# Spreading sample steps over two tiles with deeper buffer rings in a hybrid decoder layer on eight cores

The kernel runs on all 8 cores of one Trainium2 chip (two dies, cores 0 to 3 and 4 to 7); every core does its own share and no core talks to another. The metric is the device time of the slowest core, in microseconds (us). Executions come in two states: in the slow one a whole die has a lower granted TensorE clock (0.84 to 0.89 instead of 0.97 in the slow runs of the changed kernel) and the program takes 1580 to 1630 us instead of 1480.

## What is computed

One layer of a decoder, for a long prompt (one sequence of 2048 tokens for each core) and for a group of short samples (16 sequences of 4 tokens for each core), with the same weights:

```python
def decoder_layer(x, mk, mv, s0, buf, pos0, p):
    mix, s_new, buf_new = token_mix(rmsnorm(x, p['norm_mix_g']), s0, buf, pos0, p)   # gated linear attention + pooling
    h = x + mix
    h = h + cross_attn(rmsnorm(h, p['norm_x_g']), mk, mv, p['w_xq'], p['w_xo'])      # 256 memory tokens, 4 heads
    h = h + sq_relu_mlp(rmsnorm(h, p['norm_mlp_g']), p['w_up'], p['w_down'])         # 1024 -> 4096 -> 1024
    return h, s_new, buf_new
# reference(...): once for the prompt (fresh state, K/V computed from mem_prompt),
# once for the samples (state_gla, state_pool, cache_mem_k, cache_mem_v are inputs)
```

For each sample a core has to load and update one recurrent state (0.5 MiB in f32, stored back), and to load one block of keys and one of values (1 MiB each in f32, 0.5 MiB once cast to bf16).

## The kernel before

The prompt goes through in four tiles of 512 tokens. Each tile has a first part (input projections, a chunk loop for the linear attention, pooling, branch gates, output projection), the attention over the memory, and the channel mixer (eight "up" and eight "dn" units). Weights are units of 1024 x 512. They pass through five slots, `wt0` to `wt4`; a unit that comes from the f32 input `wu` is cast by its load, which POOL issues; a unit that has once been stored in bf16 (`wscratch`) is loaded plain by SP:

```python
        if name in ONCE:
            cast, store = True, False
        elif times == 0 and name[:2] != "bp":              # first use of the unit
            cast, store = True, idx % 3 == 0
        elif times == 1 and idx % 3 != 0 and name[:2] != "bp":   # second use
            cast, store = True, True
        else:
            cast, store = False, False
        if cast:
            self.dma("pool", flat, src, nb=5.6)
        else:
            self.dma("sp", flat, self.scr[idx], nb=2.5, rtok=[("scr", idx)])
        if store:
            self.dma("sp", self.scr[idx], flat, nb=2.5, wtok=[("scr", idx)])
```

The work on the samples is three generators: G (states), K (keys), V (values). The prompt's code calls `self.step("G")` and so on at chosen places; each call emits one sample's work there. Before, they were called as follows, and each used a ring of two buffers:

```python
        # up(c): after each up unit            self.step("G"); self.step("K")
        # down(c): after each token block      self.step("G"); self.step("K")
        # end of the tile                      self.drain("G"); self.drain("K")
        # first part: after each v, k, q group  self.step("V")
    def states(self):
        ...
        for i in range(SB):
            sf = self.ring("s0f", self.s0f)              # two buffers
            sb_ = self.ring("s0b", self.s0b)
            ...
            self.dma("sp", sf[...], I["sgla"][i], nb=1.4)
            self.dma("pool", sb_[...], I["sgla"][i], nb=1.4)   # the same state again, cast
            ...                                          # matmuls; sf = sf * decay + k^T v on DVE
            self.dma("sp", O["sgs"][i], sf[...], nb=1.4)
            yield
    def keys(self):                                      # values(): the same with "cv"
        for i in range(SB):
            kv = self.ring("kv", self.kv)                # two buffers
            self.dma("pool", kv[:, :], I["ckT"][i], nb=3.0)
            ...
            yield
```

The instruction streams are not written in program order. A list scheduler in the kernel simulates the five engines with the given costs and puts each engine's instructions in the order in which they start there; on the chip every engine then takes its list in that order.

Of the kernel before, what the change touches and what calls it, by code (L numbers as in the profile page):

```python
# [37 lines left out]
class Graph:  # L38

    def __init__(self, nc, stack, dry):  # L40
        self.nc = nc
        self.stack = stack
        self.dry = dry
        self.ops = []
        self.n = 0
        self.base = {}
        self.byname = {}
        self.banks = {}
        self.blkcache = {}
        self.lastw = {}  # L50
        self.readers = {}
        self.tokw = {}
        self.tokr = {}
        self.pri_off = 0
        self.coarse = []

# [40 lines left out]
    def op(self, eng, fn, reads=(), writes=(), cost=0.1, dma=False, nb=0, rtok=(), wtok=(), tab=None):  # L97
        i = self.n
        self.n += 1
        if self.dry:  # L100
            return i
        deps = {}

        def add(j, kind):
            if j != i:
                o = deps.get(j)
                if o is None or kind < o:
                    deps[j] = kind
        rb = set()
        for ap in reads:  # L110
            rb.update(self.blocks(ap))
        wb = set()
        for ap in writes:
            wb.update(self.blocks(ap))
        for t in rtok:
            rb.add(("t", t))
        for t in wtok:
            wb.add(("t", t))
        lastw, readers = self.lastw, self.readers
        for b in rb:  # L120
            w = lastw.get(b)
            if w is not None:
                add(w, 0)
            if isinstance(b, tuple) and b[0] == "p":
                for r in readers.get(b, ()):
                    if self.ops[r].eng != eng:
                        add(r, 1)
        for b in wb:
            w = lastw.get(b)
            if w is not None:  # L130
                add(w, 1)
            for r in readers.get(b, ()):
                add(r, 1)
        for b in wb:
            lastw[b] = i
            readers[b] = []
        for b in rb:
            if b not in wb:
                readers.setdefault(b, []).append(i)
        o = Op()  # L140
        o.i, o.eng, o.fn, o.deps, o.cost, o.dma, o.nb, o.tab = i, eng, fn, deps, cost, dma, nb, tab
        o.pri = i + self.pri_off
        o.succ = []
        o.ev = None
        self.ops.append(o)
        return i

    def schedule(self, window=600):
# [23 lines left out]
        while left:  # L172
# [34 lines left out]
            if o.dma:  # L207
                s = max(t + c + 1.2, dma_free)
                dma_free = s + o.nb
                o.end = dma_free + 0.8  # L210
            else:
                o.end = t + c
# [258 lines left out]
class Prog:  # L471
# [50 lines left out]
    def alloc(self):  # L522
# [37 lines left out]
        self.s0f = [g.sb(f"s0f{i}", Q + 16384 + 4096 * i, [128, 4, 256], F32) for i in range(2)]  # L560
# [36 lines left out]
        self.kv = [g.sb(f"kv{i}", Y + 9216 + 4096 * i, [128, 2048], BF16) for i in range(2)]  # L597
# [69 lines left out]
    def W(self, name):  # L667
# [14 lines left out]
        if name in ONCE:  # L682
            cast, store = True, False
        elif times == 0 and name[:2] != "bp":
            cast, store = True, idx % 3 == 0
        elif times == 1 and idx % 3 != 0 and name[:2] != "bp":
            cast, store = True, True
        else:
            cast, store = False, False
        if cast:  # L690
            self.dma("pool", flat, src, nb=5.6)
        else:
            self.dma("sp", flat, self.scr[idx], nb=2.5, rtok=[("scr", idx)])
# [88 lines left out]
    def vcost(self, eng, out, ins, simple):  # L782
        n = self.nfree(out)
        if eng == "pool":
            return 0.2 + 0.00184 * n
        if simple and not any(self.is_ps(i) for i in ins):
            return 0.13 + 0.00063 * n
        return 0.13 + 0.00109 * n
# [38 lines left out]
    def dma(self, q, out, in_, nb=None, rtok=(), wtok=()):  # L827
        if nb is None:
# [3 lines left out]
                         cost=0.75 if q == "pool" else 0.07, dma=True, nb=nb, rtok=rtok, wtok=wtok)  # L832
# [9 lines left out]
    def consts(self):  # L842
        I = self.I
        d = self.dma
        for t, n in ((self.cols, "cols"),):
            d("sp", t[:], I[n][:, :])
        d("sp", self.bmk[:], I["c_bmk"][:, :])
# [24 lines left out]
    def consts4(self):  # L872
        I = self.I
        d = self.dma
        d("pool", self.smask[:], I["c_smask"][:, :])
# [5 lines left out]
    def program(self):  # L881
        I = self.I
        self.consts()
        self.gen = {}
        self.pend = None
        for s in range(4):
            self.dma("sp", self.land[s][:, :], I["xp"][s * 128:(s + 1) * 128, :])
        for s in range(4):
            self.norm_in(s)
# [12 lines left out]

    def norm_in(self, s):
        self.xnn = getattr(self, "xnn", {})
        self.xnn[s] = None
# [52 lines left out]
    def tile(self, ti):  # L958
# [4 lines left out]
        self.hooks = {}  # L963
        if ti >= 1:
            self.sample_hooks(ti)
        us = [(ti * 4 + s) % 5 for s in range(4)]
        b = self.bank()
        self.mm(self.pb[b][:16, :], [(self.wgz[:, kc, :], A[:, kc, :]) for kc in range(8)])
        self.cp("act", self.gzT[:, :], self.pb[b][:16, :])
        self.hook("gz")  # L970
        if first:
            self.consts2()
        u = self.W("v0")

        def vgroup(u, n, s):
# [3 lines left out]
            self.step("V")  # L979
        vgroup(u, 0, 0)  # L980
        for h in range(4):
# [10 lines left out]
        for s in range(1, 4):  # L992
            vgroup(u, 0, s)
        self.hook("v", 0, u)
        u = self.W("v1")
        for s in range(4):
            vgroup(u, 1, s)
        self.hook("v", 1, u)
        for nm, dst, E in (("k", self.kd, self.E1), ("q", self.qi, self.E2)):
            u = self.W(nm)  # L1000
            for h in range(4):
# [3 lines left out]
                self.step("V")  # L1005
            self.hook(nm, u)
        og = [self.W("og0"), self.W("og1")]
        u0 = self.W("u0")
        if first:
            self.consts3()  # L1010
            self.gen["pre"] = self.precompute()
# [17 lines left out]
        for c in range(4):  # L1029
# [47 lines left out]
            pend = (o2, c)  # L1077
            if first:
                self.step("pre", 2)
# [3 lines left out]
        for s in range(4):  # L1083
            uproj(u1, 1, s)
            if s == 1:
# [23 lines left out]
        if first:  # L1109
            self.consts4()  # L1110
        for n in range(2):
            ug = self.W(f"gb{n}")
            uw = self.W(f"bp{n}")
            for m in range(4):
# [6 lines left out]
                self.stt("dve", self.t1[:, m, :], t[:, :], 1.0, self.pb[b2][:, :], ALU.add, ALU.mult)  # L1121
            self.hook("b", n, ug, uw)
# [4 lines left out]
            for m in range(4):  # L1127
# [8 lines left out]
                self.tt("dve", self.mT[:, n * 4 + m, :], t2[:, :], self.t1[:, m, :], ALU.add)  # L1136
            self.hook("a", n, ug, uw)
            if first:
                self.step("pre", 4)
        if first:  # L1140
            self.drain("pre")
        for s in range(4):
# [18 lines left out]
        def C_(s):  # L1161
# [14 lines left out]
            for hp in range(2):  # L1176
                self.tt("pool", Pn[:, 2 * hp:2 * hp + 2, :], pf[hp][:, :].rearrange("p (h m) -> p h m", m=256),
# [23 lines left out]
        for f, s in ((O_, 0), (O_, 1), (O_, 2), (T_, 0), (O_, 3), (T_, 1), (C_, 0), (T_, 2), (C_, 1), (T_, 3), (C_, 2), (PT_, 0),  # L1201
                     (C_, 3), (X_, 0), (PT_, 1), (X_, 1), (PT_, 2), (M_, 0), (X_, 2), (PT_, 3), (M_, 1), (X_, 3), (M_, 2)):
            f(s)
            if f is O_ and s == 3:
                self.hook("o", uo)
        hs = {}
# [6 lines left out]
        def up(c):  # L1213
            h = hs[c] = self.ring("hid", self.hid)
            for j in range(2):
# [19 lines left out]
                self.step("G")  # L1235
                self.step("K")

        def down(c, each=None):
            h = hs[c]
            ud = [self.W(f"dn{c}_0"), self.W(f"dn{c}_1")]  # L1240
            for s in range(4):
# [7 lines left out]
                self.step("G")  # L1249
# [26 lines left out]
        if ti == 0:  # L1276
            self.drain("P")
        down(2, nxt)
        down(3, last)
        self.drain("G")  # L1280
# [201 lines left out]
    def states(self):  # L1482
# [22 lines left out]
        for i in range(SB):  # L1505
            sf = self.ring("s0f", self.s0f)
# [4 lines left out]
            self.dma("pool", sb_[:, :, :].rearrange("p h v -> p (h v)"), I["sgla"][i], nb=1.4)  # L1511
# [26 lines left out]
    def keys(self):  # L1538
# [14 lines left out]
        for i in range(SB):  # L1553
            kv = self.ring("kv", self.kv)
            kT = kv[:, :].rearrange("p (j m) -> p j m", m=256)
            self.dma("pool", kv[:, :], I["ckT"][i], nb=3.0)
# [28 lines left out]
    def values(self):  # L1585
        I = self.I
        bo = self.hold(1)[0]
        for i in range(SB):
            kv = self.ring("kv", self.kv)
            vv = kv[:, :].rearrange("p (a d) -> p a d", d=1024)  # L1590
            self.dma("pool", kv[:, :], I["cv"][i], nb=3.0)
# [93 lines left out]
```

## Time and profile before

| | before |
|---|---|
| median of all 20 runs (5 of them slow), us | 1594.3 |
| profiled fast run, spans of the cores | 1566.7 to 1607.8 |
| slowest core in it | core 6 |

The page of the profile gives busy times and the make-up of the chain of work that ended last.

```profile
PE 1360.1 (85%) x7848; PEld 664.3 (41%) x7848; DVE 642.1 (40%) x1105; ACT 462.6 (29%) x931; POOL 207.2 (13%) x284
...
PE 64%; DMA 25%; DVE 3%; issue 3%; ACT 2%; POOL 1%; SPq 1%; POOLq 0%; DVEq 0%; ACTq 0%
```

Read it so: TensorE (PE) is busy 85% of the span, and a quarter of the chain is transfers, which end the idle time of PE. Where that quarter lies is in the lines that the prediction shows.

For the comparison I cut each core's span at matmuls that every version has: the first matmul on the gate columns (`wgz`), the first matmul of each tile's attention (on `WqK`), and the first 384-column "up" matmul of each tile.

### The profile page before, as it was taken

The page shows a single profiled execution, that of the slowest core. Times are in us where ns is not written, and L with a number is a line of the kernel's source. Part 1 is how long each engine was busy: PE and PEld are TensorE (multiplying, and loading weights), DVE is VectorE, ACT ScalarE, POOL GpSimd, SP SyncE. Part 2 cuts the span into 40 slices and gives each one's busy share as a digit, 9 for nine tenths or more (in the row PEclk, how much of TensorE's full clock was granted, in tenths as well). Part 3 has the DMA queues.
Part 4 walks back from the last instruction along what each step waited for, and adds up shares of the span by engine and source line. Part 5 has one row for each costly group of instructions (what it writes and reads, how often), then busy time and mean ns, then how long its engine had stood idle before and what let it go on. Part 6 is the DMA issues. An engine that isn't in the chain of part 4 may idle for free.

```text
span 1607.8 us, 21667 instructions; the slowest of 8 cores (1566.7 to 1607.8 us)
## 1 busy us (share of the span) xinstructions
PE 1360.1 (85%) x7848; PEld 664.3 (41%) x7848; DVE 642.1 (40%) x1105; ACT 462.6 (29%) x931; POOL 207.2 (13%) x284
## 2 busy tenths in 40 slices
PE   0883988999999989973889999999977369999997
PEld 0341533444445435431334545444433235454443
DVE  1361233543545235532365523534415033354334
ACT  1251321522246216210115512521114033152111
POOL 3121010300102003100010200300111121020000
PEclk9997999999999999985889999999988679999887
DMA  9969799769894797889976314445879833411321
GB/s 210 171 130 192 152 217 183 184 131 174 219 225 143 195 203 237 192 211 247 225 247 216 129 53 137 126 137 191 190 131 255 146 104 145 158 53 70 114 105 60
DMA packets 49252, 265.59 MB, mean 165 GB/s; under 512 B 6294, under 2 KB 6750, under 8 KB 25452
## 3 DMA queue, kind: packets, MB, share of 16 engines
q0 software_dynamic: 18336, 93.77, 36.0%
q1 hardware_dynamic: 30812, 170.43, 29.9%
q8 instruction: 65, 1.06, 0.3%
q14 instruction: 39, 0.32, 0.1%
HBM read 302.31 MB, written 56.36 MB: 223 GB/s over the span
## 4 chain that ended last, share of the span: by engine, by line
PE 64%; DMA 25%; DVE 3%; issue 3%; ACT 2%; POOL 1%; SPq 1%; POOLq 0%; DVEq 0%; ACTq 0%
PE pb L725 58%; DMA wt_45<-wu 4%; PE pb L736 3%; DMA pmf<-wpmT 2%; DMA kv_131<-cv 2%; PE pb L755 2%; DMA kv_131<-ckT 2%; DMA sgs<-s0f_85 2%; DMA wt_46<-wu 2%; DMA wt_43<-wscratch 2%; DMA s0f_84<-sgla 2%; DMA wscratch<-wt_46 1%; DMA wt_43<-wu 1%; PE pb L746 1%; DMA s0b_116<-sgla 1%
## 5 line engine op out<-in xcount | busy, mean ns | idle before, releaser
L791 DVE TENSOR_TENSOR xh<-pb,xh 128x512 f32<-128x512 f32 x160 | 110.3, 690 | 140.1 <-PE pb L725 139.8
L791 POOL TENSOR_TENSOR stat<-stat,ncols 128x1 f32<-128x1 f32 (+2 forms) x87 | 59.2, 686 | 569.5 <-DVE stat L797 569.5
L779 ACT ACTIVATE tmp_86<-pb 128x512 f32<-128x512 f32 (+2 forms) x66 | 38.8, 588 | 249.1 <-PE pb L725 219.6
L725 PE MATMUL pb<-actT,wt_46 128*128 128x512 bf16 (+2 forms) x472 | 102.3, 372 | 3.2 <-DVE actT L791 2.2
L725 PE MATMUL pb<-actT,wt_45 128*128 128x512 bf16 (+2 forms) x408 | 89.1, 369 | 4.1 <-DVE actT L791 2.8
L725 PE MATMUL pb<-actT,wt_44 128*128 128x512 bf16 (+2 forms) x376 | 81.5, 369 | 8.3 <-DMA wt_44<-wu 4.5
L779 ACT ACTIVATE tmp_88<-pb 128x512 f32<-128x512 f32 (+2 forms) x67 | 39.4, 587 | 169.6 <-PE pb L725 126.2
L725 PE MATMUL pb<-actT,wt_43 128*128 128x512 bf16 x320 | 73.2, 385 | 0.0
L725 PEld LDWEIGHTS pb<-actT,wt_46 128*128 128x128 bf16 x472 | 45.0, 98 | 56.2 <-issue 10.2
L725 PE MATMUL pb<-actT,wt_47 128*128 128x512 bf16 (+2 forms) x312 | 65.5, 363 | 2.1 <-DVE actT L791 1.5
L725 PE MATMUL pb<-wt_43,actT 128*128 128x512 bf16 x224 | 56.2, 404 | 10.0 <-DMA wt_43<-wscratch 9.1
L779 ACT ACTIVATE tmp_89<-pb 128x512 f32<-128x512 f32 (+2 forms) x59 | 34.6, 586 | 97.6 <-PE pb L725 84.9
L779 ACT ACTIVATE tmp_87<-pb 128x512 f32<-128x512 f32 (+2 forms) x58 | 34.0, 586 | 94.9 <-PE pb L725 79.1
L725 PEld LDWEIGHTS pb<-actT,wt_45 128*128 128x128 bf16 x408 | 38.4, 98 | 48.1 <-issue 8.0
L725 PE MATMUL pb<-WqK,actT 128*128 128x512 bf16 x256 | 57.9, 379 | 0.0
L725 PEld LDWEIGHTS pb<-actT,wt_44 128*128 128x128 bf16 x376 | 35.4, 98 | 48.6 <-issue 10.4
L755 PE MATMUL pb<-ident,xn_90 128*128 128x128 bf16 x176 | 14.6, 231 | 48.2 <-DVE xn_90 L797 28.5
L725 PEld LDWEIGHTS pb<-actT,wt_43 128*128 128x128 bf16 x320 | 31.5, 99 | 38.4 <-issue 4.6
L725 PE MATMUL pb<-wt_47,hid_59 128*128 128x512 bf16 x192 | 46.7, 389 | 0.0
L725 PE MATMUL pb<-wt_44,actT 128*128 128x512 bf16 x192 | 44.2, 379 | 0.2 <-DVE ogs_93 L802 0.2
L725 PEld LDWEIGHTS pb<-actT,wt_47 128*128 128x128 bf16 x312 | 29.0, 98 | 34.0 <-issue 3.0
L791 DVE TENSOR_TENSOR actT<-pb,cols 128x1024 bf16<-128x1024 bf16 x32 | 38.9, 1218 | 9.3 <-PE pb L755 9.3
(466 smaller groups left out, 2350.6 us busy)
## 6 DMA issues: line engine op xcount, KB each, us to landing
wt_46<-wscratch SPq DMA_DIRECT2D x18, 1024.0 KB
wt_45<-wscratch SPq DMA_DIRECT2D x17, 1024.0 KB
wt_44<-wscratch SPq DMA_DIRECT2D x16, 1024.0 KB
wt_47<-wscratch SPq DMA_DIRECT2D x16, 1024.0 KB
wt_43<-wscratch SPq DMA_DIRECT2D x15, 1024.0 KB
wt_43<-wu POOLq DMA_DIRECT2D x14, 1024.0 KB, 16.5
wt_44<-wu POOLq DMA_DIRECT2D x14, 1024.0 KB, 15.9
wt_45<-wu POOLq DMA_DIRECT2D x14, 1024.0 KB, 15.1
```

What stands on the lines that cost most here:

```text
L725: ins = e.matmul(out, l, r, start=(start and i == 0), stop=(stop and i == m - 1))
L736: ins = e.matmul(out, l, r, start=(i == 0), stop=(i == m - 1))
L746: ins = e.matmul(out, l, r, start=False, stop=last and k == len(al) - 1)
L755: ins = e.transpose(o, i, d)
L779: return self.g.op("act", lambda e: e.activation(out=out, in_=in_, func=func, scale=scale, **kw), reads=rd, writes=wr, cost=c, tab=tab)
L791: return self.g.op(eng, lambda e: e.tensor_tensor(out=out, in0=in0, in1=in1, op=op), reads=[in0, in1], writes=[out], cost=self.vcost(eng, ...
```

## The change

The intent is to take the sample transfers off the path that sets the end: each ring gets four to six buffers in place of two, and their steps are spread, so that a transfer has the time of several steps. Its core, shortened:

```diff
-        self.s0f = [... 2 buffers]
+        self.s0m = [... 4 buffers]          # in the mixer of tile 1
+        self.s0a = [... 4 buffers]          # in the first part of tile 2
-        self.kv = [... 2 buffers]
+        self.kvm = kv + [3 more]            # keys
+        self.kva = kv + [4 more]            # values
...
-        elif times == 0 and name[:2] != "bp":
-            cast, store = True, idx % 3 == 0
-        elif times == 1 and idx % 3 != 0 and name[:2] != "bp":
-            cast, store = True, True
+        elif name[:2] == "bp":
+            cast, store = False, False
+        elif times == 0 or (times == 1 and name[:2] != "up"):
+            cast, store = True, times == 1 or name[:2] == "up"   # tile 0 stores the up units, tile 1 the rest
...
+        if ahead is not None:               # a transfer may not be ordered more than `ahead` us of PE work
+            k = bisect.bisect_right(self.pelog, (self.peclk - ahead, 1 << 60)) - 1
+            if k >= 0:                      # before its place: 60 for weights, 30 for the rest
+                deps[self.pelog[k][1]] = 0
...
-            self.dma("pool", sb_[...], I["sgla"][i], nb=1.4)
+            self.cp("act", sb_[:, :, :], sf[:, :, :])        # the bf16 copy from SBUF, on ACT
...
-                self.step("G")                               # up: each unit
+                if c + j:
+                    self.step("G")
-                self.step("G")                               # down: each token block
+                if s % 2 == 0:
+                    self.step("G")
+            self.step("V")                                   # new: one in each chunk of tile 3, and in its gates
+            self.step("G")                                   # new: the rest of the states in tile 2's first part
...
-                self.tt("pool", Pn[...], ...)
+                self.tt("dve" if hp else "pool", Pn[...], ...)   # half of the softmax scaling on DVE
```

Not shown: the order of loads at the start (the first unit `v0` is used before the gate chain, small tables leave the first 60 us, "the first minute"), that the states of the mixer's last two `down` parts may use only the last two of the four buffers (`s0m[2:]`), and new cost figures for the scheduler. The part with `ahead` is called the lookahead below.

## The prediction

> **What bounds the kernel now.** I read the slices of the page first, to see where TensorE is not busy.
>
> ```profile
> PE   0883988999999989973889999999977369999997
> ...
> PEclk9997999999999999985889999999988679999887
> DMA  9969799769894797889976314445879833411321
> ```
>
> One digit is 40 us. PE is at 9 for most of the span; the holes are slices 0 to 3, 17 to 20 and 29 to 32, and in all three the DMA row is high. Next I cut the span into stages, with the windows view of core 6: to 283 is the first prompt tile until its output projection, 325:435 its channel mixer, 435:600 the first part of tile 1, 641:830 the mixer of tile 1 with the sample states, 1202:1330 the change to tile 3 with the sample values.
>
> ```profile
> core 6: us, PE busy (x) PEld busy (x) DVE busy (x) ACT busy (x) POOL busy (x), PEclk, DMA share, GB/s
> 0.00:283.00 283.00, 197.22 (x1041) 96.25 (x1042) 93.14 (x158) 81.26 (x157) 49.23 (x74) 0.93 0.91 179
> ...
> 325.00:435.00 110.00, 109.42 (x554) 50.84 (x552) 51.11 (x73) 23.50 (x40) 10.64 (x17) 1.00 0.86 181
> 435.00:600.00 165.00, 153.93 (x872) 74.23 (x871) 65.64 (x116) 61.76 (x127) 18.78 (x22) 0.98 0.79 190
> ...
> 641.00:830.00 189.00, 137.55 (x651) 62.75 (x650) 78.05 (x163) 23.77 (x47) 20.93 (x33) 0.82 0.87 220
> 830.00:1202.00 372.00, 346.32 (x2144) 174.36 (x2144) 158.23 (x269) 113.88 (x229) 40.63 (x53) 0.98 0.51 151
> 1202.00:1330.00 128.00, 76.30 (x590) 39.36 (x591) 42.17 (x75) 37.38 (x85) 21.30 (x28) 0.75 0.72 172
> 1330.00:1590.00 260.00, 254.77 (x1473) 122.41 (x1472) 100.76 (x162) 67.34 (x131) 17.56 (x23) 0.94 0.27 99
> ```
>
> PE busy times clock is work at full speed; the stage less that is loss: 100 us to 283; 7 in 283:435 and 600:641 together; 14 in 435:600; 76 in 641:830; 33 in 830:1202; 71 in 1202:1330; 18 after that, taken on core 0, whose clock was 0.99 there. Loss 319, work 1270, together about the 1590 of a fast run. So PE bounds the stages with no loss, and three DMA stalls make 247 of the 319 us. The chain and the waits say what they are:
>
> ```profile
> 4.95 35.70 DMA pmf<-wpmT
> 40.98 3.37 issue
> 47.04 1.23 DVE actT L791
> 48.51 34.16 PE pb L725 x148
> ...
> 714.66 21.72 DMA sgs<-s0f_85
> 736.45 9.99 DMA s0f_85<-sgla
> ...
> 1280.40 4.99 DMA kv_131<-cv
> 1286.63 6.44 DMA kv_131<-cv
> ```
>
> ```profile
> POOL pmT L791 <- DMA pmf<-wpmT: 22.6, 1, 22.6
> ```
>
> The first matmuls of any length start at 48.5 us: POOL, strictly in order, sits on the multiply of pmf (landed at 40.7), and behind it stands the reciprocal root for the fourth token block. Later, two-buffer rings take turns: a state buffer is loaded, updated, stored, reloaded; a value buffer is loaded and used.
>
> ```profile
> q0 software_dynamic: 18336, 93.77, 36.0%
> q1 hardware_dynamic: 30812, 170.43, 29.9%
> ```
>
> 36.0% of 1607.8 us over 93.77 MB: a 1 MiB weight unit cast from f32 costs 6.5 us of all 16 DMA engines; in the same way a plain load or store of one costs 3.0. One unit feeds PE for 32 matmuls of 0.216 us, 6.9 us. So cast plus store (9.5) is slower than PE, cast alone just keeps up.
>
> **What the Trainium skill says.** "DMA: Bandwidth & Descriptors", section "SWDGE vs HWDGE vs iDMA": a cast must be issued from GpSimd; the trace agrees, all loads from wu are on POOL's queue. The same page, "Issuing engines are not separate DMA queues": all queues end on the same 16 engines; agreed, shares of both queues add to 1.0 in saturated stages. Its "Bandwidth" table has 6.15 us for 1 MB; the 6.5 us above, for bytes written, is close and is used. "TensorE: Matmul & The Clock Gate", "What's actually happening": the array halves its clock after an idle window of some 3.4 us. The trace agrees: clock 0.75 in 1202:1330. A stall therefore costs more than its length, and removing one returns more.
>
> **The change, part by part.** PE's matmul count is unchanged (7848); only when they may run changes.
>
> *Start.* In the instruction listing POOL now does four reciprocal roots before pmT, and the pooling constants, sample history and smaller tables leave the first minute (about 1.2 MB of casts, 7.7 us, plus a 0.7 MB copy and one store, 5). Unit v0 landed at 23.7 (its store was issued then); the fourth unit, q, at 54.9, now about 42, og0 then at 48.5. PE runs v0, v1, k, q (27.6 us) from 23.7 to 51 and takes og0, which began at 80.8 before: 30 us earlier.
>
> *Rest of tile 0's first part.* From about 90, when the chunk loop (81 to 122 before, so some 40 us from 51) frees its slots, 17 casts (110) plus pooled weights, memory outputs, reloaded x and constants (30) give 140 us of DMA, and weight stores there (3 x 3.0, one of which held its slot for 20 us in the chain) go. The last unit lands at 230 and feeds about 10 us of matmuls: end near 240, not 283: **-43** in all, loss 57.
>
> *Mixer of tile 0.* All 8 up units are stored here against 5 of 16 before: +9 us of DMA, mostly under 110 us of PE. **+3**.
>
> *Tile 1, first part.* Before: 11 units cast and stored, 5 plain. Now 16 cast and stored: 5 x 3.5 + 5 x 3.0 = 32 us more DMA, in all about 170 (with x and y) for 151 us of work. Four or five units come early, so I book **+11**.
>
> *Tile 1, mixer and states.* Weights: 8 casts with stores instead of 11, -20 us. States: 16 x (1.5 load + 1.5 store + 1.6 second, casting load) = 74 us becomes 14 x 3.0 = 42, two states going to tile 2. Before, a state took (821-648)/16 = 10.8 us. With four buffers the cycle of about 14 us of load, update and store allows one each 4; PE work between steps is 110/15 = 7.3. DMA still carries about 132 us for 125 of PE, so loss 20 instead of 76: **-56**. The bf16 copy on ACT is 16 x 1.05 us, on an engine busy 24 of 189 us.
>
> *Keys and values.* Five and six buffers instead of two, values over 18 steps instead of 16 in a row. 0.5 MiB cast takes 3.2 us of DMA, PE work between steps about 7, so landing time (6.5) hides. Tile 2: 33 to 20, **-13**. Tile 3's start: 71 to 12, **-59**.
>
> *Softmax half from POOL to DVE.* 16 x 0.69 us on a DVE busy about half of those stages: 0.
>
> Sum: -43+3+11-56-13-59 = -157; 1590-157 = 1433. I add 17 us, a chosen allowance for POOL and SP: weight loads now wait there for stores of their slot, ahead of POOL work that PE needs. **Predicted 1450 us.**
>
> **Rivals.** (1) *The stall moves to tile 1*: 16 stored units in a row, each holding its slot, POOL stuck between them. For: in the chain one store of a slot cost 20 us, and DMA is at 0.79 there already. Against: five slots are 34 us of PE work. If so, tile 1 loses 40 to 60 more: about 1500. (2) *The whole is DMA volume in tile 0*, which the change hardly cuts: the early start then only waits later for weights. For: share 0.91 up to 283. Against: PE is idle until 48 and DMA has holes (0.6 and 0.7) in slices 2 and 4. Then 25 of the 43 vanish: 1475. (3) *A dense PE lowers the clock.* Core 6 ends at 0.81 over its last 70 us with PE busy; more time in that state costs 20 to 40 us. Against: 283:435 ran dense at 1.00 on it. (4) *The lookahead is too short*: waits for state or key tiles grow. Against: 30 us is above the 6.5 us landing.
>
> **Range and chances.** Low end: nearly no loss outside tile 0, 1405. High end: rivals 1 or 2 with some of 3, 1505. Even both together leave it 4% below before; slower would need a new stall of over 150 us. Faster 0.95, same 0.04, slower 0.01.
>
> **What would show it right or wrong.** Long matmuls from about 24 us and no POOL wait on pmf before the roots; tile 0's output projection done near 240; loss of at most 25 us in the part of tile 1 where all weights are cast and stored, with DMA share near 1; state waits on sgla and sgs mostly gone from the chain; PE at 9 with clock near 1 where the values were. Wrong would be: PE waiting for wt tiles behind store completions, or POOL roots late in tile 1.

## The result

| | before | after |
|---|---|---|
| median, us | 1594.3 (20 runs, 5 slow) | 1480.2 (10 runs, 3 slow) |
| lowest, us | 1588.6 | 1477.1 |
| profiled run, spans of the cores | 1566.7 to 1607.8 | 1447.0 to 1481.2 |
| mean of the eight spans | 1588.9 | 1461.8 |

Outputs are correct. The ratio of after to before is 0.9284, with a 95% interval of 0.9267 to 0.93. Here and below a ratio is the mean time of one kernel's fast runs over that of the kernel before in the same rounds on the same chip, so it is not quite the ratio of the medians. The class (faster) and the range of the prediction held; the point, 1450, was 30 us too low.

The page of the kernel after, first the slices (37 us each; core 3, the slowest), then busy times and the chain:

```profile
PE   3987969899988979999988999989989989999996
...
PEclk9999989999999999998999999999999999999998
DMA  9959999689989599567996215528387995511341
...
PE 1336.4 (90%) x7848; PEld 657.3 (44%) x7848; DVE 649.4 (44%) x1121; ACT 478.8 (32%) x947; POOL 188.2 (13%) x254
...
PE 72%; DMA 18%; DVE 3%; issue 2%; ACT 2%; POOL 1%; SPq 1%; DVEq 0%; POOLq 0%; ACTq 0%
```

Both later holes of the PE row have closed to 8s and 9s, the clock row no longer drops to 5 or 6, and transfers have fallen from 25 to 18% of the chain. The first hole has shrunk from 0, 8, 8, 3 to 3, 9, 8, 7.

The windows view of core 6, the core that the prediction had cut up, with the columns as there (window, PE, PEld, DVE, ACT, POOL busy, clock, DMA share, GB/s): the first part of tile 0, its mixer, the first part of tile 1, the mixer of tile 1 with the states, up to the end of tile 2, the first part of tile 3 with the values, the rest.

```profile
0.00:241.00 241.00, 193.83 (x1051) 94.99 (x1052) 90.21 (x158) 80.08 (x156) 46.73 (x72) 0.96 0.96 183
276.00:385.00 109.00, 107.32 (x550) 51.15 (x551) 52.19 (x78) 23.49 (x40) 13.07 (x20) 1.00 0.87 166
385.00:562.00 177.00, 165.00 (x943) 79.86 (x941) 73.25 (x127) 67.15 (x136) 21.88 (x29) 0.99 0.91 222
598.00:770.00 172.00, 157.64 (x791) 72.64 (x791) 89.12 (x178) 49.38 (x70) 11.75 (x17) 0.93 0.84 251
770.00:1105.00 335.00, 320.86 (x2018) 163.57 (x2017) 145.87 (x257) 103.22 (x219) 38.08 (x48) 0.98 0.51 150
1105.00:1263.00 158.00, 147.12 (x1040) 75.50 (x1039) 71.31 (x121) 59.66 (x123) 26.23 (x35) 1.00 0.80 211
1263.00:1447.00 184.00, 166.39 (x1064) 82.08 (x1062) 82.96 (x131) 48.77 (x99) 11.17 (x14) 0.98 0.23 88
```

With the prediction's own measure, stage less PE busy times clock, the losses are 55, 2, 14, 25, 21, 11 and 21 us. The prediction had booked 57 for the first part of tile 0, 20 for the states, 20 for tile 2 and 12 for the start of tile 3. On this core these four lines came out nearly as booked. The first part of tile 1 did not: 25 us of loss were booked (14 and 11 more), and it stayed at 14.

The long transfers in the chain of core 6 (start, length):

```profile
3.42 21.80 DMA meml<-mem
...
157.94 30.38 DMA wt_43<-wu
...
517.28 38.44 DMA wscratch<-wt_45
...
694.31 26.98 DMA sgs<-s0f_87
721.36 11.49 DMA s0f_87<-sgla
...
1142.55 15.57 DMA va_144<-cv
```

State buffers still take turns in it, values appear once instead of again and again, and a new piece stands at the start, the memory input `meml`. The longest piece is the store of a weight unit, which holds its slot in the first part of tile 1.

Mean over the eight cores, us, of the stretches between the marks (the gate matmul is G; A0 to A3 are the first attention matmuls of the tiles, M0 to M3 the first "up" matmuls):

| stretch | before | after | difference | booked |
|---|---|---|---|---|
| start to G | 47.2 | 21.6 | -25.6 | |
| G to A0: tile 0, first part | 236.2 | 224.4 | -11.8 | -43 with the line above |
| A0 to M0 | 35.4 | 35.6 | +0.2 | |
| M0 to A1: mixer of tile 0, tile 1 first part | 281.2 | 292.1 | +10.9 | +14 |
| A1 to M1 | 36.2 | 35.7 | -0.5 | |
| M1 to A2: mixer of tile 1, states, tile 2 first part | 357.2 | 314.7 | -42.5 | -56 |
| A2 to M2 | 41.1 | 44.6 | +3.5 | 0 |
| M2 to A3: keys, values | 369.9 | 307.5 | -62.4 | -72 |
| A3 to M3 | 35.4 | 36.2 | +0.8 | 0 |
| M3 to end | 149.1 | 149.5 | +0.4 | 0 |

Before, core 6 had a clock near 0.81 over its last 97 us, which lengthened its last stretch to 160.9 (146.0 on cores 0 to 5, 156.0 on core 7); after, no core shows that. Cores 4 and 5 had the same clock before, for some 180 us between 54 and 262, so that their G to A0 took 249.8 and 241.6 us where the other six took 230.9 to 234.9 (mean 233.0): about 3 of the 11.8 us in that line are this clock and not the change. In the opposite direction the last stretch is some 3 us longer than the 146.0 of undisturbed cores. It comes with the sample part: x5 below, which undoes that part, is back at 145.7 on seven cores, and x10, which has it alone, is at 149.2. Why is open. The 3.5 us of A2 to M2 come with the scheduler's new cost figures: x6 and x10, which have the old ones, take 41.6 and 41.1.

**The cores part in pairs.** After, cores 0, 2, 5, 6 ended at 1447 to 1452 and cores 1, 3, 4, 7 at 1470 to 1481: one of each neighbouring pair is fast and one slow. In other fast runs the two change places (1447.0 and 1472.3 for cores 0 and 1 in one, 1479.5 and 1443.3 in another), while the mean of the pair mostly stays near 1460. The time of the kernel is the slow one's. The pairs parted before the change too, by 2 to 29 us in the profiled run (1607.8 on core 6, 1578.6 on core 7). Cores 3 and 6 differ by 12 us up to A0 (252.5 against 240.6) and by 14 between M0 and A1 (300.0 against 285.8), by 3 each in the states' and the values' stretch: so they part mainly where DMA is at 0.9 and more. "HBM Reference", section "Specifications (TRN2)", of the Trainium skill says that the two cores of a pair share the bandwidth of one memory stack. That fits with which cores pair up; that memory bandwidth is what they share unequally, no run here shows. The GB/s of the windows count the bytes as they are written, after the cast. An estimate with the f32 bytes that casting loads read counts POOL's queue twice: in the first 241 us of core 6 that queue moved 30.91 MB and SP's 13.14, which makes 311 GB/s; in 385:562 and 598:770 it is 308 and 293, nearer to the 358 that the page names for each core than the 166 to 251 of the windows.

### The profile page after: what moved, and what is told of

Read it like the earlier page. It is cut to its first block, busy times and chain, and to the rows that moved or that the text cites. A ratio compares the mean times of both kernels' runs of the same rounds, so it can differ in the third digit from the quotient of the medians.

```text
span 1481.2 us, 21671 instructions; the slowest of 8 cores (1447.0 to 1481.2 us)
## 1 busy us (share of the span) xinstructions
PE 1336.4 (90%) x7848; PEld 657.3 (44%) x7848; DVE 649.4 (44%) x1121; ACT 478.8 (32%) x947; POOL 188.2 (13%) x254
## 4 chain that ended last, share of the span: by engine, by line
PE 72%; DMA 18%; DVE 3%; issue 2%; ACT 2%; POOL 1%; SPq 1%; DVEq 0%; POOLq 0%; ACTq 0%
PE pb L739 65%; PE pb L750 4%; DMA wt_43<-wu 3%; PE pb L769 2%; DMA s0f_85<-sgla 2%; DMA meml<-mem 2%; DMA sps<-tmp_94 2%; DMA sgs<-s0f_84 1%; DMA wt_46<-wu 1%; PE pb L760 1%; DMA va_144<-cv 1%; DMA wt_44<-wu 1%; DMA yp<-xh 1%; DMA wt_47<-wu 1%; DMA kv_137<-ckT 1%
## 5 line engine op out<-in xcount | busy, mean ns | idle before, releaser
L739 PE MATMUL pb<-actT,wt_44 128*128 128x512 bf16 (+2 forms) x440 | 97.1, 376 | 6.9 <-ACT tmp_94 L793 4.0
L739 PE MATMUL pb<-actT,wt_43 128*128 128x512 bf16 (+2 forms) x376 | 85.8, 381 | 18.5 <-DMA wt_43<-wu 15.2
L739 PE MATMUL pb<-actT,wt_46 128*128 128x512 bf16 (+2 forms) x408 | 91.0, 376 | 8.8 <-DMA wt_46<-wu 5.5
L739 PE MATMUL pb<-actT,wt_45 128*128 128x512 bf16 (+2 forms) x344 | 73.2, 368 | 4.7 <-DVE stat L811 1.5
L739 PEld LDWEIGHTS pb<-actT,wt_44 128*128 128x128 bf16 x440 | 42.4, 100 | 56.8 <-issue 11.8
L739 PE MATMUL pb<-wt_44,actT 128*128 128x512 bf16 x256 | 63.8, 396 | 4.3 <-DMA wt_44<-wu 2.8
L739 PEld LDWEIGHTS pb<-actT,wt_46 128*128 128x128 bf16 x408 | 39.0, 100 | 53.7 <-issue 13.7
L739 PE MATMUL pb<-wt_47,actT 128*128 128x512 bf16 x192 | 45.5, 385 | 4.1 <-DVE xn_98 L816 2.5
L739 PE MATMUL pb<-wt_45,actT 128*128 128x512 bf16 x160 | 40.3, 402 | 2.3 <-ACT T_66 L793 1.1
```

The costliest lines, as they stand in the source:

```text
L739: ins = e.matmul(out, l, r, start=(start and i == 0), stop=(stop and i == m - 1))
```

## The experiments

Twelve kernels ran, in three groups that each shared the runs of the kernel before on one chip. All gave correct outputs. The stretches are means over eight cores of the profiled run, all of them in the fast state. Each comes from one execution, and the chips differ: the fast runs of the kernel before have a mean span of 1590 us in the group of x1, x2, x5 and x10, 1581 in that of x3, x4, x6 and x12, and 1586 in that of x7, x8, x9 and x13; the kernel after was run outside these groups. So 2 or 3 us between stretches of different groups mean nothing. x6, x10 and x12 have only two fast runs each. The profiled run of x3 is a long one of its kind: 1520.0 on average over the cores, where its other fast runs have 1510.6 to 1511.8.

| kernel | ratio to before, 95% | G at | G-A0 | M0-A1 | M1-A2 | M2-A3 | mean span |
|---|---|---|---|---|---|---|---|
| before | 1 | 47.2 | 236.2 | 281.2 | 357.2 | 369.9 | 1588.9 |
| after | 0.9284 (0.9267 to 0.93) | 21.6 | 224.4 | 292.1 | 314.7 | 307.5 | 1461.8 |
| x10 before, with rings and spread only | 0.9345 (0.9278 to 0.9413) | 48.7 | 235.8 | 285.8 | 316.5 | 301.3 | 1484.6 |
| x5 after, sample part undone | 0.9816 (0.975 to 0.9881) | 22.2 | 230.1 | 296.1 | 332.5 | 380.5 | 1560.6 |
| x3 after, two buffers each | 0.9605 (0.9559 to 0.9651) | 21.7 | 225.7 | 294.2 | 337.6 | 339.6 | 1520.0 |
| x4 after, steps at old places | 0.9488 (0.9459 to 0.9518) | 21.5 | 226.5 | 291.8 | 310.2 | 346.9 | 1498.9 |
| x1 after, no lookahead | 0.9323 (0.9263 to 0.9382) | 22.2 | 231.0 | 306.4 | 314.2 | 303.4 | 1478.4 |
| x2 after, stores as before | 0.9401 (0.9361 to 0.9441) | 22.2 | 242.6 | 285.4 | 324.4 | 307.7 | 1488.3 |
| x6 after, old cost figures | 0.9399 (0.9359 to 0.944) | 31.2 | 224.2 | 298.8 | 315.4 | 311.5 | 1478.8 |
| x12 after, softmax scaling on POOL | 0.9276 (0.9228 to 0.9323) | 21.6 | 223.8 | 291.7 | 313.5 | 306.4 | 1458.9 |
| x7 after, memory input later | 0.9314 (0.9274 to 0.9353) | 30.7 | 218.4 | 295.4 | 315.6 | 306.7 | 1468.3 |
| x8 after, og and u0 stored in tile 0 | 0.9296 (0.9276 to 0.9316) | 21.7 | 233.4 | 291.7 | 317.7 | 308.3 | 1473.8 |
| x9 x7 and x8 | 0.9325 (0.9291 to 0.936) | 30.9 | 223.2 | 292.4 | 315.7 | 306.1 | 1470.5 |
| x13 x9, two edits more | 0.927 (0.9252 to 0.9288) | 30.2 | 225.0 | 292.2 | 311.2 | 308.0 | 1469.3 |

### Which part brings the gain: the sample part alone, and all but it

x10 takes the kernel before and gives it only the deeper rings, the spread steps and the copy on ACT:

```diff
+        self.s0m, self.s0a, self.kvm, self.kva = ...   # deep rings
+        ...                                            # step places of the change
-            self.dma("pool", sb_[...], I["sgla"][i], nb=1.4)
+            self.cp("act", sb_[:, :, :], sf[:, :, :])
```

> The complement: the kernel before with only the sample work changed (deeper rings, steps over two tiles, bf16 copy on ACT); no lookahead, old store rule, old start. Theory: the two sample stretches fall to 310 to 325 and 305 to 320 us, the start stays as before (attention of tile 0 at about 282); total 1480 to 1505, so about 95 to 110 us faster than before. Rival (the gain needs the lookahead, without which deep rings load too early and crowd the weights): above 1530.

x5 is the opposite: the changed kernel with two buffers, the old step places and the second, casting load of each state.

```diff
-{"m": self.s0m, "u": self.s0m[2:], "a": self.s0a}
+{"m": self.s0m[:2], "u": self.s0m[2:], "a": self.s0a[:2]}
-            kv = self.ring("kvm", self.kvm)      # the same for kva
+            kv = self.ring("kvm", self.kvm[:2])
-            self.cp("act", sb_[:, :, :], sf[:, :, :])
+            self.dma("pool", sb_[...], I["sgla"][i], nb=1.4)
 ...                                              # steps of G and V as before
```

> The changed kernel with only the sample work put back: two buffers for states, keys and values, all steps where they were, the second casting load of the states. Theory (the sample rings and their spread bring about 107 of the 114 us): the stretch from the mixer of tile 1 to the attention of tile 2 goes back from 316 to about 355 us, the one from the mixer of tile 2 to the attention of tile 3 from 310 to about 365; total 1570 to 1595. Rival (the lookahead and the new queue figures order the transfers well enough that two buffers would do): below 1520.

The sample part alone gives a ratio of 0.9345, the rest alone 0.9816, everything 0.9284. So the sample part is worth 6.6% of the 7.2, the rest 1.8; the two sum to 8.4, 1.2 points more than the whole. The intervals, 0.7 points on each and about 1.0 together, hardly leave room for simple adding, so the two seem to overlap a little. By stretches the split is clean but for the states: x10 has the gains of the states and values (357 to 317 and 370 to 301) and none at the start (G at 48.7); x5 has the gain at the start. It also keeps 25 of the 42 us of the states' stretch without any deeper ring (about 355 was expected, 332.5 came), which must come from order, lookahead or stores; x2 below gives some 10 of these to the stores. Why the values' stretch of x5 is 11 us longer than that of before I did not find out.

### Depth or spread

x3 keeps the spread but has two buffers in each ring (the first part of the diff of x5). x4 keeps the rings but calls the steps where they were:

```diff
-                if c + j:
-                    self.step("G")
+                self.step("G")
...
-            self.step("V")          # in the chunk loop, the pooling input and the gates
```

> The changed kernel with the steps spread as changed, but two buffers each for states, keys and values. Theory (spread and depth share the gain: with a step every 7 us two buffers with a landing of 6.5 us nearly keep up for keys and values, while a state's cycle of about 14 us just misses): states' stretch 315 to 325-335, values' stretch 307 to 312-325, total 1.0 to 2.5% above the changed kernel. Rival (depth is what counts): both stretches as before, 355 and 370, total above 1560. Second rival (depth is worth nothing once spread): within 0.5%.

> The changed kernel with the deep rings, but every step where it was before (states in tile 1's mixer, values in a row at the start of tile 3). Theory: 16 value loads of 3.2 us of DMA in about 85 us of matmuls need most of the DMA there, six buffers cover the first third: values' stretch 307 to 320-335; states' stretch 315 to 320-335; total 1.5 to 3.5% above the changed kernel. Rival (depth alone suffices): within 0.7%.

| stretch | neither (x5) | spread only (x3) | depth only (x4) | both (after) |
|---|---|---|---|---|
| states, M1-A2 | 332.5 | 337.6 | 310.2 | 314.7 |
| keys and values, M2-A3 | 380.5 | 339.6 | 346.9 | 307.5 |

For keys and values, depth and spread are each worth 32 to 41 us, with or without the other: they add. For the states, depth does everything (22 to 23 us) and the spread costs 4 to 5. (x5 also has the second load, so its states' cell holds one difference more; and as the run of x3 is a long one, up to 9 us of its two cells may be its own. The cost of the spread rests on x4, and on x13 against x9 below, 315.7 to 311.2 on one chip.) Both theories expected too little from what was taken away for the values, 312 to 325 in x3 and 320 to 335 in x4, and x4's too much for the states, 320 to 335. The reason is in the transfers' own times. The values, from the list of DMA issues of core 3 in the stretch of keys and values (last column: median us from issue to landing), before:

```profile
kv_130<-cv POOLq DMA_DIRECT2D x8, 512.0 KB, 5.8
```

after:

```profile
kv_137<-cv POOLq DMA_DIRECT2D x3, 512.0 KB, 14.7
...
va_143<-cv POOLq DMA_DIRECT2D x2, 512.0 KB, 20.2
```

The same load takes two to three times as long from its issue (the medians of the six buffers are 10.4 to 20.2 us, those of the two before 5.8 and 6.2), most likely as more of them are under way together and beside weight loads. Six buffers cover that, as PE has several steps of some 7 us in the meantime. PE's waits for values on core 3 (us in total, times, longest), before:

```profile
PE pb L736 <- DMA kv_131<-cv: 17.2, 6, 3.6
PE pb L736 <- DMA kv_130<-cv: 15.6, 5, 3.9
```

after:

```profile
PE pb L750 <- DMA va_144<-cv: 2.7, 1, 2.7
```

A value's buffer is free once it is used. A state's buffer is not: it has to be stored first, and that store waits in the same crowd. One of the four state buffers, followed in SP's timeline of core 3 (start of the issue):

```profile
705.75 0.33 SPq L845 DMA_DIRECT2D s0f_87<-sgla  x1
...
731.21 0.39 SPq L845 DMA_DIRECT2D sgs<-s0f_87  x1
...
752.17 0.33 SPq L845 DMA_DIRECT2D s0f_87<-sgla  x1
...
781.09 0.42 SPq L845 DMA_DIRECT2D s0f_87<-sgla  x1
```

From load to load 46 us, then 29; the second time falls in the part that has only two buffers. Load and update take 25 us, the store 21. Four buffers at 46 us give a state each 12 us, two at 29 one each 14, where PE has one step each 7. In the chain of core 3 (start, length) the store of one buffer and the load of another are the longest transfers of this stage:

```profile
692.10 21.89 DMA sgs<-s0f_84
...
721.79 26.89 DMA s0f_85<-sgla
```

Part of the cycle may be SP's own line: between 690 and 790 us SP, which issues these transfers one after the other, stood 39.6 us on stores of states, 17.4 on PE, and 12.5 on the landing of a weight unit in `wt_43`. No run separates the two.

### The lookahead

```diff
-        if ahead is not None:
+        if False:
```

> The changed kernel without the lookahead, so that a transfer may be issued as soon as its buffer is free. Theory: the lookahead only keeps constants and sample loads out of the weights' way; the first minute gets about 12 us of transfers back, the rest hardly moves: 1480 to 1498. Rival (holding transfers back is what makes the two-tile spread work): above 1510. Second rival (holding back costs more than it saves): below 1475.

Without it the ratio is 0.9323, 0.4 points worse, but the intervals overlap. The stretches say where: 7 us in G-A0 and 14 in M0-A1, where DMA is saturated and an early transfer probably takes the place of a needed one; in the values' stretch it is 4 us better without, which x13 below could not get by freeing the key and value loads. On the mean of the cores the lookahead is worth 17 us (1478.4 and 1461.8); the slowest core, which makes the time, gains less, as the cores of a pair lie closer together without it.

### The stores

```diff
-        elif times == 0 or (times == 1 and name[:2] != "up"):
-            cast, store = True, times == 1 or name[:2] == "up"
+        elif times == 0:
+            cast, store = True, idx % 3 == 0
+        elif times == 1 and idx % 3 != 0:
+            cast, store = True, True
```

> The changed kernel with the old rule for which units are cast and stored in which tile. Theory (moving the stores loads the first part of tile 1 with 32 us more transfers and costs about 14 us there on the slow cores, and saves some 10 in tile 0's first part and 10 in tile 1's mixer): the stretch from tile 0's mixer to tile 1's attention falls from 300 to 283 to 290, the start rises by 5 to 10, total within 12 us of 1480. Rival (the store move is a net gain): above 1495.

My reading that the move of the stores costs on balance fell. With the old stores tile 0's first part is 18 us longer and the states' stretch 10, and only 7 come back in M0-A1; the ratio is 1.2 points worse. Five of the units stored there have 3.0 us of store each, 15 us in all, in a stage where DMA has no room, so most of the 18 are what the volume says; the held slots may be the rest.

### The scheduler's figures

```diff
-                s = max(t + c + 1.4, dma_free)
-                dma_free = s + o.nb * 1.08
-                o.end = dma_free + 1.8
+                s = max(t + c + 1.2, dma_free)
+                dma_free = s + o.nb
+                o.end = dma_free + 0.8
...                                     # and the old costs of small POOL operations and POOL issues
```

> The changed kernel with the scheduler's old figures for transfers and POOL, so only the order of instructions on each engine differs. Theory (the figures decide where POOL, ACT and SP stand in line; with optimistic landings an engine is put to wait on a late transfer): 5 to 25 us slower, seen as new waits of POOL or ACT on transfers; the attention of tile 2 goes back from 45 to 41 us if the figures made it longer. Rival (the order hardly depends on them): within 4 us.

The program is the same set of instructions; only their order differs. It costs 1.15 points: the gate comes 10 us later (31.2) and M0-A1 is 7 us longer. The attention of tile 2 is back at 41.6, so the new figures had made it longer, as the theory had allowed for. In the prediction these figures have no term at all.

### The softmax half

```diff
-                self.tt("dve" if hp else "pool", Pn[...], ...)
+                self.tt("pool", Pn[...], ...)
```

> The changed kernel with both softmax halves on POOL again. Theory (booked as nothing): total within 4 us; the attention stretches stay at 35.6, 35.7, 44.6, 36.2. Rival (the half on DVE delays the DVE work that frees PE in the attention of tile 2, which grew from 41 to 44.6): that stretch returns to 41.

Ratio 0.9276 against 0.9284, stretches equal within 2 us: it is worth nothing, as booked.

### The start: is it the wait that the chain names?

After, PE starts on `v0` at 33.0 us on core 3 rather than at 24. POOL's roots come early as foreseen, but ACT stands in line. ACT's timeline of core 3:

```profile
29.28 1.06 ACT L793 ACTIVATE Mtm_102<-meml 128x1024 bf16<-128x1024 f32 x1 [13.03 <-DMA meml<-mem]
```

Only after this does ACT evict the gate (`gzT`, at 31.38), on which PE's next matmuls wait. x7 holds the loads of the memory and of the pooled weights back, so that the scheduler puts that work later:

```diff
-        self.dma("sp", self.meml[:, :, :], I["mem"]...)
-        self.dma("sp", self.pmf[:, :], I["wpmT"][:, :])
+        self.dma("sp", self.meml[:, :, :], I["mem"]..., ahead=15.0)
+        self.dma("sp", self.pmf[:, :], I["wpmT"][:, :], ahead=15.0)
```

> The changed kernel with only the loads of the memory input and of the pooled weights held back (15 us lookahead), so that ACT evicts the gate before it works on the memory and POOL has nothing to wait for at the start. Theory (my step for the start failed because ACT, not POOL, stood in line on the memory input, 25 us on core 3): the wait of ACT for the memory leaves the first 60 us, og0 comes at about 53 us instead of 63, and the stage from the first gate matmul to the attention of tile 0 gets 6 to 10 us shorter of 224 (mean of cores); ratio to before about 0.923 against 0.928. Rival (tile 0 is DMA volume): the earlier work only waits later for weights, the stage stays within 3 us, ratio 0.928.

The wait is gone, and nothing is gained: G and G-A0 together take 249.1 us against 246.0, the ratio is 0.9314. PE's timeline of core 3 shows why. After, the first block of `og0` (in slot `wt_47`) and the next one on a new unit (in `wt_43`):

```profile
63.25 1.89 PE L739 MATMUL pb<-wt_47,actT 128*128 128x512 bf16 x8
68.89 1.89 PE L739 MATMUL pb<-wt_43,actT 128*128 128x512 bf16 x8
```

With x7, the first block of `og0` and the next one on a new unit:

```profile
52.99 1.89 PE L739 MATMUL pb<-wt,actT 128*128 128x512 bf16 x8
...
69.13 3.57 PE L739 MATMUL pb<-wt,actT 128*128 128x512 bf16 x8 [12.49 <-DMA wt<-wu]
```

`og0` runs 10 us earlier, at the place where the prediction had it, and then PE waits 12.5 us for a unit that lands at 69. The load of that unit, the second one behind `og0`, in the list of DMA issues of core 3 (last column: us from issue to landing), issued at 50.15 us after:

```profile
wt_44<-wu POOLq DMA_DIRECT2D x1, 1024.0 KB, 18.2
```

and at 39.88 with x7:

```profile
wt<-wu POOLq DMA_DIRECT2D x1, 1024.0 KB, 29.0
```

Issued 10 us earlier, it lands at the same time, 68.9 instead of 68.3. The DMA share of the first 60 us is 0.97 and 0.98 in the two: the start is mostly a question of bytes, and the longest piece in the chain was not its cost. Some of x7's wait is order: the load before that one landed at 62.5, but PE's list has its unit behind.

### Tile 1: volume or slots?

x8 stores `og0`, `og1` and `u0` in tile 0, where these units hold their slots through the whole chunk loop anyway, and loads them plain in tile 1.

```diff
-        elif times == 0 or (times == 1 and name[:2] != "up"):
-            cast, store = True, times == 1 or name[:2] == "up"
+        elif times == 0 or (times == 1 and name[:2] not in ("up", "og") and name != "u0"):
+            cast, store = True, times == 1 or name[:2] in ("up", "og") or name == "u0"
```

> The changed kernel with og0, og1 and u0 stored in tile 0, where they hold their slots through the chunk loop anyway, and loaded plain in tile 1. Theory (tile 1's first part is DMA volume): there 3 x (6.5 - 3.0) for the casts and 3 x 3.0 for the stores leave tile 1, 19.5 us of DMA, and 9 us of stores enter tile 0: the stretch from the up matmuls of tile 0 to the attention of tile 1 falls from 292 by 10 to 15, tile 0's first part grows by 0 to 6; ratio about 0.921. Rival (what tile 1 loses is latency of slots and of the tail of 16 small stores, not volume): both stay within 3 us, ratio 0.928.

Tile 0's first part grows by 9.0 us, as much as the three stores take of DMA: there the volume counts. (In x9, added to x7, the same stores cost 5.0.) M0-A1 stays at 291.7, so the 19.5 us taken out of it bought nothing. The windows of a slow core of a pair over the first part of tile 1 (last columns: clock, DMA share, GB/s), after, core 3:

```profile
400.00:590.00 190.00, 169.34 (x943) 80.87 (x942) 73.63 (x127) 69.24 (x138) 21.40 (x28) 0.96 0.89 215
```

and x8, core 2 (there core 3 is the fast one):

```profile
400.00:590.00 190.00, 171.42 (x952) 81.21 (x951) 75.00 (x127) 65.91 (x135) 20.14 (x26) 0.96 0.80 198
```

The DMA share falls from 0.89 to 0.80, the work of PE in the same 190 us rises by 2; over all cores it is 0.90 to 0.81, and 174.0 to 175.1 us. In tile 1 the volume does not bound. What does is perhaps the five slots: in the chunk loop, from about 495 to 506 us on core 3, DMA moves almost nothing (3 and 13 GB/s in two slices of 5.5 us) while units wait for a slot, POOL's next load is issued at 504 when PE lets one go, and three loads go out within 4 us of each other. A sixth slot would test it; there is no room for one, so this stays argued. A rival stands untested beside it, the small stores to `sps`: on core 3 a piece of 23.1 us in the chain from 512 us is one of them, and PE stood 4.0 us on ACT's tile `tmp_94`, which they empty, against 13.7 us on cast weights between 330 and 600.

### Both, and a last candidate

x9 is x7 and x8 together. x13 adds the state steps at their old places (from x4) and takes the lookahead off the key and value loads (from x1).

> Both edits above. Theory: they add, as they act in different stages: 14 to 22 us below the changed kernel, ratio to before 0.915 to 0.920. Rival (volume in tile 0 takes back the earlier start once stores lie there too): no better than the better of the two.

> Both edits above, the state steps at their old places (one for each up unit and each token block, since bunched steps cost nothing in the states' stretch: 310 against 315), and the key and value loads freed of the lookahead (303 against 307 without any). Theory: another 4 to 8 us below x9, ratio 0.911 to 0.916. Rival: those differences were noise or belonged to other loads; equal to x9 within 0.3 per cent.

x9 is no better than either (0.9325). x13 is half a point better than x9, and the states' stretch is 4.5 us shorter (315.7 to 311.2, as x4 had promised), though in the profiled runs other stretches give 3 of these back; freeing the key and value loads gave nothing (306.1 and 308.0), so the better values' stretch of x1 is noise or belongs to other loads. At 0.927 it is level with the change (0.9284) within the intervals. No version that ran beats the changed kernel clear of noise.

## Why the prediction was right, and where it was not

- **Start and tile 0, -43.** On core 6 the mark A0 moved from 283.4 to 240.6, which is -43; over all cores -37, some 3 of it the low clock of cores 4 and 5 before. But the step that led there failed: "PE runs v0, v1, k, q from 23.7 to 51 and takes og0". ACT's line made it 63 on core 3 and 60 on core 6. x7 showed that this had little price, since the units behind it land when DMA allows. The size came from the DMA sums in the second half of the argument (17 casts and the rest, less stores), and x2 and x8 support it: 15 and 9 us of stores put into this stage cost 18 and 9 us (5 on top of x7). Rival 2, volume in tile 0, had the right mechanism and the wrong conclusion: the change had cut enough volume for nearly the whole gain.
- **Mixer of tile 0, +3.** Core 6 loses 1.7 us there and lost 0.6 before: small, as booked.
- **Tile 1, +11.** M0-A1 grew by 10.9 on average with 14 booked for both, but that is luck: on core 6, for which it was booked, it went from 286.2 to 285.8, and on cores 1, 3, 4 and 7, the slow ones of their pairs, it grew by 10 to 25. The step behind it failed as well: I derived it from 32 us more of DMA, and x8 took 19.5 of DMA out for nothing. Rival 1 (40 to 60 more) did not come in the time, though its mechanism is there: between 330 and 600 us POOL stood 25.7 us on stores of slots on core 6 (6.3 on core 3), and one such store is the 38.4 us piece of the chain, but PE lost only 7.9 us to weights there.
- **States, -56.** Measured -42.5 (-46 on core 6). The failing step is "with four buffers the cycle of about 14 us": it was 46 on four buffers and 29 on two, with single loads and stores of 22 and 27 us in the chain. I had taken landing times measured with two transfers under way and used them with four to eight. The loss of 20 has no clear source either: its 132 us of DMA and 125 of PE do not follow from the lines shown, by which 0.87 of 189 us less 20 and 32 leaves 112 of DMA, and 137.55 us at 0.82 are 113 of PE. The spread of the states, part of my reason, is even slightly harmful (x4, and x13 against x9).
- **Keys and values, -72.** Measured -62 (-64 on core 6). "Landing time (6.5) hides" is right in its conclusion and wrong in its number: it became 10 to 20 us and is hidden all the same, since five or six buffers cover it: on every core PE's waits for these loads fell from 40 to 44 us to 4 to 8. Here depth and spread each bring half.
- **Softmax half, 0.** x12: right.
- **The allowance of 17 us** for POOL and SP behind stores was not needed for that. What it had to cover had no term: I cut up one core and took it for the slowest. Core 6 fell by 160 us, from 1607.8 to 1447.6, some 12 of it the lower clock at its end that did not come back; the 157 of the sum is 9 us more than the 148 that are left. So close it is partly by luck: on that core tile 1 cost none of the 14 booked, states and values brought 10 and 8 less than booked, and A2 to M2 took 4 more. The time is that of the slow core of a pair. Core 6 was the slow one of its pair before and the fast one after; core 3, slow in both, fell by 114. Core 3 ended 34 us after core 6, 12 of them up to A0 and 14 in M0-A1, the stages that are full of DMA, and that is the whole of the 30 us by which 1450 was too low. Why one core of a pair is later in them was not tested.
- **Rival 3, a dense PE lowers the clock,** did not come in fast runs: the last stage of every core took 148.7 to 150.3 us. **Rival 4, too short a lookahead:** x1 shows at most 4 us for the values against 21 that it saves elsewhere.

## What to carry to other kernels

Give a ring as many buffers as the landing time under its own load needs, and count it again after deepening: with six buffers a load landed in 10 to 20 us where it landed in 6 with two, and a buffer that must be stored before it is free pays that twice. Before removing the wait that stands longest in the chain, ask when the next unit lands. In the stage with a DMA share of 0.96 bytes counted; in the one with about 0.9, taking out 19.5 us of them bought nothing. Predict for the slowest core, not for the one that happens to be on the page: here one core of each pair ended 20 to 34 us before the other.

## What the Trainium skill lacked or had wrong

- "HBM Reference", section "Specifications (TRN2)", gives each core of a pair half of the stack's bandwidth when both stream. These runs show an uneven result: one core of a pair mostly ends at 1439 to 1454 us and the other at 1466 to 1481, changing places from run to run, at an estimated 293 to 311 GB/s of core 6 in its full stages. The page has nothing on unequal shares; the cause was not tested here.
- "TensorE: Matmul & The Clock Gate", section "Seeing it yourself", says to budget 13/16 of the clock once three cores of a die run dense matmuls. In the fast profiled run all eight cores were dense from 288 to 384 us (PE busy 93.6 to 96.0 of 96) at a granted clock of 0.99 to 1.00. The lower clock came in some executions only: 0.84 to 0.89 on average over one die in the slow runs, and about 0.81 in the profile of before, for some 180 us on cores 4 and 5 and for 66 and 97 us near the end of cores 7 and 6, not on all four cores of that die at once.
- "DMA: Bandwidth & Descriptors", section "Bandwidth", has 6.15 us and 341 GB/s for a single transfer of 1 MB, though 1 MB in 6.15 us is about half that rate. Here plain transfers cost 2.8 us of the 16 engines per MB (29.9% of 1607.8 us over 170.43 MB), which fits the rate and not the time. The 6.2 us per MB written by casting loads (36.0% over 93.77 MB), which the prediction set beside the 6.15, are alike by chance, as such a load reads 2 MB of f32 for each. The section gives no time from issue to landing under load, and that is what a ring's depth follows from: 5.8 us before and 10 to 20 us after for the same 0.5 MiB load.
